# One product per tile of 32 keys: the operands of a level stage laid together in one tile

## The chip, the cores and the metric

The kernel runs on one core of a Trainium2 chip. The metric is the device time of one launch in microseconds (us), the median of several runs. Five engines work at once, each through its own queue in order: PE multiplies matrices (its weight loads are listed apart, as PEld), DVE, ACT and POOL do elementwise work, SP starts transfers (DMA).

## The reference, cut to what matters

The model has one layer: RMSNorm, a combined input projection, a causal pooling branch and a gated linear recurrence, a gated merge, an output projection, then a gated feed-forward part. The change lies in the recurrence alone, which is computed for 4 heads of 128 channels over 2048 positions:

```
q = silu(zq);  f = lb + (1 - lb) * sigmoid(zf);  k = 1 - f;  v = zi
S_t = diag(f_t) S_{t-1} + k_t v_t^T
o_t = S_t^T q_t
```

Written over a chunk of positions this is `attn[t, s] = sum_c q[t, c] * k[s, c] * prod(f[s+1..t, c])` for s <= t, then `o = attn v` plus a term from the state at the chunk's start.

## The kernel before, in words

All large products are done in float32 that is split in a high and a low part (three products for one), and in two-level form with seven partial products P1 to P7 instead of eight. The sequence is worked in two rounds (`b` = 0 and 2) of 1024 positions, as two halves of `TB` = 512. A round is a mixer (projections, recurrence, pooling, merge) and a feed-forward part (up projection, convolution, down projection). The weights come through a stream of raw tiles that SP loads; ACT casts the high part and DVE subtracts the low part. In round 0 the kernel also makes the sums of weights that the seven-product form needs, in DRAM, by large accumulating transfers (class `Sums`).

The recurrence of one head and one half is `hgrn_task`, a Python generator. It is stepped by `tick`, once for every 6 large products that the kernel emits, so its instructions stand between those of the projections; `yield AHEAD` puts 3 ticks between making the operands and using them. The two halves of a head run as a pair and share every place: a **group** below means the products of both halves at one place. There are 4 heads in each of 2 rounds, so 8 pairs. A scheduler sets the final order on every engine; `in_turn` pins a group to its place in PE's stream.

A half has `NT` = 4 chunks of 128 positions. Instead of dividing by decays, `hgrn_task` builds the 128x128 matrix of a chunk in four **level stages** (`hh` = 1, 2, 8, 32). At each, queries are multiplied by the decay up to a block's border (`d`, `f` in the profile) and keys by the decay behind it; `q`, `k` and `d` are updated in place for the next stage. Stages 1, 2 and 8 fill the diagonal tiles of 32 keys (`GK` = 32, `NG` = 4 tiles per chunk); stage 32 fills the blocks between the tiles.

For each stage `operands` gives two tiles: `qn` with the near queries in two parts of 64 columns a chunk, and `qf` with one further part. `products` multiplies, for each chunk, each part (`s`) and each key tile `g`, 32 columns of keys (the weights) with 32 columns of `qn`, or with 16 of `qf`. The four key tiles write four different quarters of the PSUM partitions, `ps[g * GK : g * GK + GK]`. After that `put` copies the wanted elements under a mask into `at` (DVE), and stage 32 copies blocks with ACT. Products of this part are plain float32; the profile lists two matmuls and two weight loads for each.

All these tiles, like nearly everything else in SBUF, come from one pool `slots` of 77 buffers of 512 (528) columns. A buffer is given out again when its last reader is done, which can be a transfer that stores it.

Of the kernel before, what the change touches and what calls it, by code (L numbers as in the profile page):

```python
# [11 lines left out]
F32 = mybir.dt.float32  # L12
# [3 lines left out]
ALU = mybir.AluOpType  # L16
AX = mybir.AxisListType

P = 128
# [38 lines left out]

M_ORDER = (0, 4, 1, 5, 2, 6, 3, 7)

N_SLOTS = 77
N_RUN = 3
N_HEADS = 2
GO_AT = 3
# [21 lines left out]
def tile_trunk(  # L86
# [20 lines left out]
    rawp = ctx.enter_context(tc.tile_pool(name="rawp", bufs=N_RAW))  # L107
    opsp = ctx.enter_context(tc.tile_pool(name="opsp", bufs=N_OPS))
    slots = ctx.enter_context(tc.tile_pool(name="slots", bufs=N_SLOTS))
    dram = ctx.enter_context(tc.tile_pool(name="dram", bufs=1, space=bass.MemoryType.DRAM))  # L110
    banks = ctx.enter_context(tc.tile_pool(name="banks", bufs=8, space=bass.MemoryType.PSUM))

    def slot(name, cols=TB, dt=F32):
        return slots.tile([P, cols], dt, tag="s", name=name, padded_shape=[P, 528])
# [513 lines left out]
    def setup_task():  # L628
        scratch = [hist.rearrange("p a b -> p (a b)")[:, :64], uhist.rearrange("p a b -> p (a b)")]

        def mask_of():
            scratch.reverse()
            return scratch[0]

        keys = [(h, h, 0, h) for h in (1, 2, 8)]
        keys += [(8 * h + t, 2 * h, t * h, h) for h in (2, 8) for t in range(2)]
        for key, x, off, w in keys:
            nb = 64 // x
            mf = mask_of()
# [20 lines left out]
        masks[0] = m8.unsqueeze(2)  # L660
# [339 lines left out]
    def hgrn_task(b, h, d, q, vd, zd, od):  # L1000
# [20 lines left out]
        def products(hh, near, far):  # L1021
            x = GK // 2
            pa_ = bank(f"pl{b}_{h}_{hh}", NT * 3 * x)
            ps = pa_.rearrange("p (c x) -> p c x", c=NT)
            for c in range(NT):
                for s in range(2):
                    for g in range(NG):
                        o = ps[g * GK : g * GK + GK, c]
                        ins = pe.matmul(
                            o[:, 2 * x :] if s else o[:, : 2 * x],  # L1030
                            ks[:, c * P + g * GK : c * P + g * GK + GK],
                            far[:, c, g * x : g * x + x] if s else near(c, g),
                            start=True, stop=True)
                        if not (c or g or s):
                            in_turn(ins)
# [12 lines left out]
        qn, qf = operands(1)  # L1048
        act.copy(qn.rearrange("p c s x -> p (c s x)"), q)
        dve.tensor_tensor(qf, qo, do, ALU.mult)  # L1050
        dve.tensor_tensor(qe, qe, de, ALU.mult)
        dve.tensor_tensor(qo, qf, de, ALU.mult)
        yield AHEAD
        flat = qn.rearrange("p c s x -> p c (s x)")
        ps = products(1, lambda c, g: flat[:, c, g * GK : g * GK + GK], qf)
        yield 2
        dve.copy_predicated(ac, masks[0].rearrange("p x o -> p o x").to_broadcast([P, NT, GK]),
                            ps[:, :, :GK])
# [5 lines left out]
        for hh in (2, 8, 32):  # L1064
# [4 lines left out]
            qn, qf = operands(hh)  # L1069
            half = qn[:, :, 1].rearrange("p c (b t h) -> p c b t h", t=2, h=hh)  # L1070
            act.copy(qn[:, :, 0].rearrange("p c (b h) -> p c b h", h=hh),
                     qv.rearrange("p c (b t h) -> p c b t h", t=2, h=hh)[:, :, :, 1, :])
            act.copy(half[:, :, :, 0, :], q5[:, :, :, 2, :])
# [3 lines left out]
            f4 = qf.rearrange("p c (b h) -> p c b h", h=2 * hh)  # L1077
            dve.tensor_tensor(f4, qn[:, :, 1].rearrange("p c (b h) -> p c b h", h=2 * hh),
                              d5[:, :, :, 1, 0:1].to_broadcast(full), ALU.mult)
            dve.tensor_tensor(q2, f4, d5[:, :, :, 0, 0:1].to_broadcast(full), ALU.mult)  # L1080
            yield AHEAD
            if hh < GK:
                x = GK // 2
                ps = products(hh, lambda c, g: qn[:, c, :, g * x : g * x + x], qf)
                yield 1
                put(halves(hh), hh, ps[:, :, :x], hh)
                for t in range(2):
                    put(halves(2 * hh), 8 * hh + 1 - t, ps[:, :, (1 + t) * x : (2 + t) * x], 2 * hh)
            else:
                for g in range(NG - 1):  # L1090
                    r = slice(g * GK, g * GK + GK)
                    act.copy(av[r, :, r], ac[r])
                pa_ = bank(f"pl{b}_{h}_{hh}", NT * 96)
                ps = pa_.rearrange("p (c x) -> p c x", c=NT)
                for c in range(NT):
                    for g, to, w in ((0, slice(0, 32), qn[:, c, 0, :32]), (1, slice(0, 64), qn[:, c, 1]),
                                     (2, slice(0, 32), qn[:, c, 0, 32:]), (0, slice(32, 96), qf[:, c])):
                        ins = pe.matmul(ps[g * GK : g * GK + GK, c, to],
                                        ks[:, c * P + g * GK : c * P + g * GK + GK], w,
                                        start=True, stop=True)  # L1100
                        if not c and not g and not to.start:
# [897 lines left out]
```

## Time and profile before

| what | value |
|---|---|
| time, median of 3 runs (range) | 2491.97 us (2491.5 to 2494.51) |
| time of the profiled execution | 2491.93 us |
| span of that execution | 2490.1 us, granted PE clock 0.997 |
| busy: PE, PEld, DVE, ACT, POOL | 2464.5, 2004.7, 1924.1, 1233.2, 780.5 us |
| matmuls on line 1029 (stages 1, 2, 8) | 1536 of 32 columns, 1536 of 16 columns |
| matmuls on line 1098 (stage 32) | 384 from qn, 128 from qf |

The time around the span is 1.8 us. In rows of the profile, `L1029` is a line of the kernel, `pl<-qn,k` means that the instruction writes `pl` and reads `qn` and `k` (numbers of buffers left out), and `128x32` is partitions by elements of the moving operand. A row of a timeline has the start, the time from the first start to the last end, and how many instructions were merged; in square brackets stands the time that the engine was idle before it, and what ended that.

### The profile page before, as it was taken

The page shows a single profiled execution, that of the slowest core. Times are in us where ns is not written, and L with a number is a line of the kernel's source. Part 1 is how long each engine was busy: PE and PEld are TensorE (multiplying, and loading weights), DVE is VectorE, ACT ScalarE, POOL GpSimd, SP SyncE. Part 2 cuts the span into 40 slices and gives each one's busy share as a digit, 9 for nine tenths or more (in the row PEclk, how much of TensorE's full clock was granted, in tenths as well). Part 3 has the DMA queues.
Part 4 walks back from the last instruction along what each step waited for, and adds up shares of the span by engine and source line. Part 5 has one row for each costly group of instructions (what it writes and reads, how often), then busy time and mean ns, then how long its engine had stood idle before and what let it go on. Part 6 is the DMA issues. An engine that isn't in the chain of part 4 may idle for free.

```text
span 2490.1 us, 41224 instructions
## 1 busy us (share of the span) xinstructions
PE 2464.5 (99%) x14372; PEld 2004.7 (81%) x14372; DVE 1924.1 (77%) x3318; ACT 1233.2 (50%) x2344; POOL 780.5 (31%) x1090
## 2 busy tenths in 40 slices
PE   9999999999999999999999999999999999999998
PEld 7877787887888888888888888887888888888887
DVE  7767666988899777885596766769979887778755
ACT  6535444434545545554464455453365554445534
POOL 5343352502354334461240101213033433335410
PEclk9999999999999999999999999999999999999999
DMA  8878778687898879997444343457443444447852
GB/s 274 273 198 268 213 219 249 205 251 250 200 260 232 232 222 245 262 364 249 131 157 154 114 145 120 141 161 245 147 138 123 157 145 143 148 136 248 319 165 100
DMA packets 257711, 498.03 MB, mean 200 GB/s; under 512 B 26912, under 2 KB 47520, under 8 KB 257184
## 3 DMA queue, kind: packets, MB, share of 16 engines
q1 hardware_dynamic: 189872, 317.53, 38.9%
q0 software_dynamic: 42656, 112.74, 17.7%
q10 hardware_dynamic: 24976, 65.13, 7.5%
q8 instruction: 113, 1.85, 0.3%
q14 instruction: 94, 0.77, 0.1%
HBM read 383.63 MB, written 189.27 MB: 230 GB/s over the span
## 4 chain that ended last, share of the span: by engine, by line
PE 80%; DVE 3%; DMA 2%; issue 1%; ACT 0%; POOL 0%; SPq 0%; ACTq 0%; DVEq 0%; POOLq 0%
PE dn_P L152 17%; PE up_Z L152 15%; PE up_V L152 10%; PE up_X L152 10%; PE wo_P L152 5%; PE pb L152 3%; PE gr_X L152 2%; PE gr_V L152 2%; PE io_Z L152 1%; PE gr_Z L152 1%; PE gr_Y L152 1%; PE gr_W L152 1%; PE io_V L152 1%; PE fr_X L152 1%; PE fr_V L152 1%; DVE ops L249 1%
## 5 line engine op out<-in xcount | busy, mean ns | idle before, releaser
L248 ACT CAST ops<-raw 128x512 fp32r<-128x512 f32 x792 | 487.5, 620 | 798.6 <-PE dn_P L152 180.2
L249 DVE TENSOR_TENSOR ops<-raw,ops 128x512 fp32r<-128x512 f32 x792 | 590.4, 749 | 239.3 <-ACT ops L248 229.9
L1733 DVE SCALAR_TENSOR_TENSOR e<-h,cols,e 128x512 f32<-128x512 f32 x176 | 143.1, 818 | 30.5 <-ACT e L1731 25.9
L1731 ACT ACTIVATE e<-h,cols 128x512 f32<-128x512 f32 x176 | 142.2, 814 | 25.5 <-DVE h L1181 18.8
L1736 DVE SCALAR_TENSOR_TENSOR e<-h,cols,e 128x512 f32<-128x512 f32 x176 | 133.7, 769 | 2.5
L996 POOL DMA_DIRECT2D g_P<-dg_P x154 | 84.5, 550 | 159.8 <-PE dn_P L152 113.5
L1302 POOL TENSOR_TENSOR gf_P<-e,e 128x512 f32<-128x512 f32 x44 | 61.5, 1400 | 150.4 <-DVE e L1742 96.2
L470 POOL TENSOR_TENSOR raw<-raw,raw 128x512 f32<-128x512 f32 x36 | 49.9, 1386 | 110.2 <-DVE ops L249 95.6
L1302 POOL TENSOR_TENSOR gf_P<-gf_P,e 128x512 f32<-128x512 f32 x44 | 59.1, 1343 | 72.1 <-DVE e L1742 71.6
L1726 POOL COPY h<-h 128x2 f32<-128x2 f32 x88 | 40.3, 470 | 117.0 <-DVE h L1180 107.4
L1740 ACT ACTIVATE e<-e 128x512 f32<-128x512 f32 x88 | 55.6, 632 | 38.0 <-DVE e L1736 37.8
L1728 POOL COPY hist<-h 128x2 f32<-128x2 f32 x88 | 35.9, 408 | 117.6 <-DVE h L1181 115.8
L1181 DVE TENSOR_TENSOR h<-up_u,up_V 128x512 f32<-128x512 f32 x88 | 60.0, 682 | 10.2 <-PE up_V L152 9.7
L1442 POOL TENSOR_TENSOR q<-q,qs 128x512 f32<-128x512 f32 x16 | 22.4, 1401 | 125.0 <-ACT qs L1441 125.0
L1277 DVE TENSOR_TENSOR x<-x,wo_P 128x512 f32<-128x512 f32 x88 | 55.9, 680 | 5.9 <-PE wo_P L152 5.6
L1277 DVE TENSOR_TENSOR ac<-ac,dn_P 128x512 f32<-128x512 f32 x72 | 47.1, 681 | 16.3 <-PE dn_P L152 16.1
L1475 ACT ACTIVATE gt<-gt,cols 128x512 f32<-128x512 f32 x48 | 34.8, 725 | 42.8 <-DVE gt L1181 41.5
L1221 ACT COPY up_e<-up_X 128x512 f32<-128x512 f32 x44 | 25.9, 588 | 59.3 <-PE up_X L152 56.4
L718 POOL TENSOR_SCALAR ro<-so 128x4 f32<-128x4 f32 x16 | 5.0, 311 | 156.3 <-ACT sq L1154 156.1
L1726 POOL COPY h<-hist 128x2 f32<-128x2 f32 x88 | 44.5, 513 | 28.5 <-DVE m_T42l L685 28.5
L1756 POOL DMA_DIRECT2D dg_P<-gf_P x88 | 50.7, 576 | 8.1 <-POOL gf_P L1302 7.4
L1616 POOL TENSOR_TENSOR ya<-ya,gl 128x512 f32<-128x512 f32 x24 | 36.7, 1552 | 26.2 <-DVE ya L1613 14.8
(1328 smaller groups left out, 8021.4 us busy)
## 6 DMA issues: line engine op xcount, KB each, us to landing
g_P<-dg_P POOLq DMA_DIRECT2D x154, 256.0 KB, 5.9
raw<-in_w_up_t SPq DMA_DIRECT2D x132, 256.0 KB, 3.0
raw<-in_w_in_t SPq DMA_DIRECT2D x98, 256.0 KB, 3.5
dg_P<-gf_P POOLq DMA_DIRECT2D x88, 256.0 KB, 3.9
dg_P<-e SPq DMA_DIRECT2D x66, 256.0 KB, 3.4
raw<-in_w_dn SPq DMA_DIRECT2D x66, 256.0 KB, 3.9
x<-in_x SPq DMA_DIRECT2D x64, 256.0 KB, 4.6
gd<-gt ACTq DMA_DIRECT2D x64, 256.0 KB, 3.4
```

Source lines behind the costliest of these rows:

```text
L152: count[1] = pe.matmul(*args, **kw)
L248: self.mark = act.copy(hi, v)
L249: low = self.low = dve.tensor_tensor(lo, v, f32(hi), ALU.subtract)
L996: eng.dma_start(t, d)
L1181: return dve.tensor_tensor(dst, t, ps, ALU.add if how == "add" else ALU.subtract)
L1277: dve.tensor_tensor(t, t, ps[j], ALU.add if sg > 0 else ALU.subtract)
L1302: pin(eng.tensor_tensor(t, x0, x1, op))
L1726: pool.tensor_copy(h[:, 0:2], hist[:, mt] if hf == 0 else hs[s, 0][:, TB : TB + 2])
L1731: in_turn(act.activation(t, h[:, 2:], AF.Identity, bias=col(o_cb + mt), scale=col(o_cw + 4 * MF + mt)))
L1733: in_turn(second(dve.scalar_tensor_tensor(t, h[:, 1 : 1 + TB], col(o_cw + 2 * MF + mt), t, ALU.mult, ALU.add)))
L1736: dve.scalar_tensor_tensor(t, h[:, 0:TB], col(o_cw + mt), t, ALU.mult, ALU.add)
L1740: in_turn(act.activation(g, g, AF.Silu))
```

## The change

`operands` now gives one tile `qm` with three parts of 64 columns per chunk, from a pool of its own with 3 buffers of 768 columns; `slots` goes from 77 buffers to 73. The parts are in such an order that the columns for key tile `g` are 16 of each part. `products` issues one matmul of 48 columns per chunk and key tile, where there were two of 32 and 16. In stage 32 the far part lies behind the first two, so key tile 0 takes 96 neighbouring columns in one product: three products per chunk where there were four.

With the layout some elementwise work changes shape. In stage 1 even and odd queries go to different parts, so ACT's one copy of 512 columns becomes two strided copies of 256, and the masked copy reads the product in another order. In stage 32 one ACT copy of 256 columns becomes two of 128. The other copies and multiplications write other places with the same sizes.

```diff
-N_SLOTS = 77
+N_SLOTS = 73
+N_QM = 3
...
+    qmp = ctx.enter_context(tc.tile_pool(name="qmp", bufs=N_QM))
...
         def operands(hh):
-            near = slot(f"qn{b}_{h}_{hh}").rearrange("p (c s x) -> p c s x", c=NT, s=2)
-            far = slot(f"qf{b}_{h}_{hh}")[:, : NT * 64].rearrange("p (c x) -> p c x", c=NT)
-            return near, far
+            t = qmp.tile([P, NT * 192], F32, tag="qm", name=f"qm{b}_{h}_{hh}")
+            return t.rearrange("p (c s x) -> p c s x", c=NT, s=3)
...
-                for s in range(2):
-                    for g in range(NG):
-                        o = ps[g * GK : g * GK + GK, c]
-                        ins = pe.matmul(
-                            o[:, 2 * x :] if s else o[:, : 2 * x],
-                            ks[:, c * P + g * GK : c * P + g * GK + GK],
-                            far[:, c, g * x : g * x + x] if s else near(c, g),
-                            start=True, stop=True)
+                for g in range(NG):
+                    ins = pe.matmul(ps[g * GK : g * GK + GK, c],
+                                    ks[:, c * P + g * GK : c * P + g * GK + GK],
+                                    qm[:, c, :, g * x : g * x + x], start=True, stop=True)
...
-        act.copy(qn.rearrange("p c s x -> p (c s x)"), q)
-        dve.tensor_tensor(qf, qo, do, ALU.mult)
+        qm = operands(1)
+        act.copy(qm[:, :, 0], qe)
+        act.copy(qm[:, :, 1], qo)
+        dve.tensor_tensor(qm[:, :, 2], qo, do, ALU.mult)
...
+            if hh < GK:
+                act.copy(near, qh)
+            else:
+                for i in range(2):
+                    act.copy(near[:, :, 1 - i], qh[:, :, i])
...
-                    for g, to, w in ((0, slice(0, 32), qn[:, c, 0, :32]), (1, slice(0, 64), qn[:, c, 1]),
-                                     (2, slice(0, 32), qn[:, c, 0, 32:]), (0, slice(32, 96), qf[:, c])):
+                    flat = qm[:, c].rearrange("p s x -> p (s x)")
+                    for g, (at, w) in enumerate(((96, 96), (0, 64), (64, 32))):
```

Two places show how it stands in the queues. The first is PE's queue at stage 2 of head 0 in round 0. `gr_0_X<-x_f5h` and its like are large products of the projection; `pl_0_2` is the PSUM bank of this stage, once for each half; `x4` counts neighbouring rows alike. Before (each pair of rows of one half stands four times):

```order
L152 MATMUL gr_0_X<-x_f5l,ops_1445 128x512
L152 MATMUL gr_0_X<-x_f5h,ops_1445 128x512
L1029 MATMUL pl_0_2_1649<-qn_0_2_1593,k_0_1451 32x32 x4
L1029 MATMUL pl_0_2_1649<-qf_0_2_1594,k_0_1451 32x16 x4
...
L1029 MATMUL pl_0_2_1682<-qn_0_2_1604,k_0_1464 32x32 x4
L1029 MATMUL pl_0_2_1682<-qf_0_2_1605,k_0_1464 32x16 x4
...
L152 MATMUL gr_0_X<-x_f6h,ops_1445 128x512
```

In the changed kernel the same place of PE's queue reads:

```order
L154 MATMUL gr_0_X<-x_f5l,ops_1448 128x512
L154 MATMUL gr_0_X<-x_f5h,ops_1448 128x512
L1028 MATMUL pl_0_2_1618<-qm_0_2_1564,k_0_1454 32x48 x16
L1028 MATMUL pl_0_2_1635<-qm_0_2_1574,k_0_1467 32x48 x16
L154 MATMUL gr_0_X<-x_f6h,ops_1448 128x512
```

The group stands between the same two large products; its 64 products of two sizes are now 32 of one. Over the whole program all other PE instructions keep their order, and two of the 32 groups stand one product later.

The second place is ACT's queue where the operands of stage 1 of head 0 are made, for both halves. `CAST ops` is the high part of a weight tile, `f`, `k` and `qs` belong to the recurrence, the `DMA` rows start transfers for the sums of weights. Before:

```order
L248 CAST ops_1490<-raw_1103 128x512
L1009 ACTIVATE k_0_1451<-f_0_1388 128x512
L1437 ACTIVATE f_0_1434<-f_0_1434 128x512
L1049 COPY qn_0_1_1456<-q_0_1408 128x512
L1008 ACTIVATE f_0_1434<-f_0_1434,lbt 128x512
L248 CAST ops_1578<-raw_1120 128x512
L325 DMA su0s_1358<-in_w_up_t 512x1x512
L1009 ACTIVATE k_0_1464<-f_0_1434 128x512
L1049 COPY qn_0_1_1469<-q_0_1363 128x512
L1221 COPY gr_0_e_1481<-gr_0_X 128x512
```

In the changed kernel ACT's queue at that place reads:

```order
L250 CAST ops_1493<-raw_1106 128x512
L1011 ACTIVATE k_0_1454<-f_0_1391 128x512
L1439 ACTIVATE f_0_1437<-f_0_1437 128x512
L1046 COPY qm_0_1_1459<-q_0_1411 128x4x64
L1047 COPY qm_0_1_1459<-q_0_1411 128x4x64
L1010 ACTIVATE f_0_1437<-f_0_1437,lbt 128x512
L1046 COPY qm_0_1_1472<-q_0_1366 128x4x64
L1047 COPY qm_0_1_1472<-q_0_1366 128x4x64
L250 CAST ops_1549<-raw_1123 128x512
L327 DMA su0s_1361<-in_w_up_t 512x1x512
L1011 ACTIVATE k_0_1467<-f_0_1437 128x512
L1223 COPY gr_0_e_1484<-gr_0_X 128x512
```

Two copies stand where one stood, and the second half's copies have moved ahead of a weight cast and of `k`.

More of the change, by code (lines that the diff above doesn't have):

```diff
@@ L1016, in operands, with products @@
         def operands(hh):
[L1017 to L1021 removed]
+            t = qmp.tile([P, NT * 192], F32, tag="qm", name=f"qm{b}_{h}_{hh}")
+            return t.rearrange("p (c s x) -> p c s x", c=NT, s=3)
+        def products(hh, qm):
             x = GK // 2
@@ L1047, in hgrn_task @@
         de, do = (dv.rearrange("p c (b t) -> p c b t", t=2)[:, :, :, t] for t in range(2))
-        qn, qf = operands(1)
-        act.copy(qn.rearrange("p c s x -> p (c s x)"), q)
-        dve.tensor_tensor(qf, qo, do, ALU.mult)
+        qm = operands(1)
+        act.copy(qm[:, :, 0], qe)
+        act.copy(qm[:, :, 1], qo)
+        dve.tensor_tensor(qm[:, :, 2], qo, do, ALU.mult)
         dve.tensor_tensor(qe, qe, de, ALU.mult)
-        dve.tensor_tensor(qo, qf, de, ALU.mult)
+        dve.tensor_tensor(qo, qm[:, :, 2], de, ALU.mult)
         yield AHEAD
-        flat = qn.rearrange("p c s x -> p c (s x)")
-        ps = products(1, lambda c, g: flat[:, c, g * GK : g * GK + GK], qf)
+        ps = products(1, qm)
         yield 2
-        dve.copy_predicated(ac, masks[0].rearrange("p x o -> p o x").to_broadcast([P, NT, GK]),
-                            ps[:, :, :GK])
+        dve.copy_predicated(ac.rearrange("p c (b t) -> p c b t", t=2),
+                            masks[0].to_broadcast([P, NT, GK // 2, 2]),
+                            ps[:, :, :GK].rearrange("p c (t b) -> p c b t", t=2))
         put(halves(1), 1, ps[:, :, GK:], 1)
@@ L1068, in hgrn_task @@
             q2 = qv.rearrange("p c (b t h) -> p c b t h", t=2, h=2 * hh)[:, :, :, 1, :]
[L1069 to L1072, printed above, removed]
+            qm = operands(hh)
+            qh = qv.rearrange("p c (b t h) -> p c b t h", t=2, h=hh)[:, :, :, 1, :]
+            near = qm[:, :, 1].rearrange("p c (b h) -> p c b h", h=hh)
+            half = qm[:, :, 0].rearrange("p c (b t h) -> p c b t h", t=2, h=hh)
+            if hh < GK:
[3 more added lines that the diff above has]
+                    act.copy(near[:, :, 1 - i], qh[:, :, i])
             act.copy(half[:, :, :, 0, :], q5[:, :, :, 2, :])
@@ L1076, in hgrn_task @@
             full = [P, NT, nb, 2 * hh]
[L1077 to L1080, printed above, removed]
+            f0, f1 = (qm[:, :, s].rearrange("p c (b h) -> p c b h", h=2 * hh) for s in (0, 2))
+            dve.tensor_tensor(f1, f0, d5[:, :, :, 1, 0:1].to_broadcast(full), ALU.mult)
+            dve.tensor_tensor(q2, f1, d5[:, :, :, 0, 0:1].to_broadcast(full), ALU.mult)
             yield AHEAD
@@ L1083, in hgrn_task @@
                 x = GK // 2
-                ps = products(hh, lambda c, g: qn[:, c, :, g * x : g * x + x], qf)
+                ps = products(hh, qm)
                 yield 1
-                put(halves(hh), hh, ps[:, :, :x], hh)
+                put(halves(hh), hh, ps[:, :, x : 2 * x], hh)
                 for t in range(2):
-                    put(halves(2 * hh), 8 * hh + 1 - t, ps[:, :, (1 + t) * x : (2 + t) * x], 2 * hh)
+                    put(halves(2 * hh), 8 * hh + 1 - t, ps[:, :, 2 * t * x : (2 * t + 1) * x], 2 * hh)
             else:
@@ L1095, in hgrn_task @@
                 for c in range(NT):
-                    for g, to, w in ((0, slice(0, 32), qn[:, c, 0, :32]), (1, slice(0, 64), qn[:, c, 1]),
-                                     (2, slice(0, 32), qn[:, c, 0, 32:]), (0, slice(32, 96), qf[:, c])):
[L1098 to L1101, printed above, removed]
+                    flat = qm[:, c].rearrange("p s x -> p (s x)")
+                    for g, (at, w) in enumerate(((96, 96), (0, 64), (64, 32))):
+                        ins = pe.matmul(ps[g * GK : g * GK + GK, c, :w],
+                                        ks[:, c * P + g * GK : c * P + g * GK + GK],
+                                        flat[:, at : at + w], start=True, stop=True)
+                        if not (c or g):
                             in_turn(ins)
```

6 lines of the change are left out of this document (3 added, 3 removed).

## The prediction

> **What bounds the kernel now.** I read the page's busy times and chain first, then the waits of PE, then the two mixers beside each other, then single groups. The page, parts 1, 3 and 4:
>
> ```profile
> PE 2464.5 (99%) x14372; PEld 2004.7 (81%) x14372; DVE 1924.1 (77%) x3318; ACT 1233.2 (50%) x2344; POOL 780.5 (31%) x1090
> q8 instruction: 113, 1.85, 0.3%
> PE 80%; DVE 3%; DMA 2%; issue 1%; ACT 0%; POOL 0%; SPq 0%; ACTq 0%; DVEq 0%; POOLq 0%
> ```
>
> PE sets the end: what is taken off its stream comes off the time, as long as others keep up. Its longest waits (total, times, longest), and the two mixers as stretches (length, then busy time and count for PE, PEld, DVE, ACT and POOL, granted clock, DMA share, GB/s):
>
> ```profile
> PE pl L1029 <- issue: 4.7, 3, 2.9
> PE gr_X L152 <- issue: 3.1, 1, 3.1
> PEld pl L1029 <- ACT qn L1049: 1.5, 2, 0.9
> ```
>
> ```profile
> 100.00:420.00 320.00, 308.75 (x3079) 249.92 (x3078) 219.52 (x525) 151.45 (x341) 121.86 (x117) 0.98 0.82 234
> 1350.00:1640.00 290.00, 290.00 (x3045) 238.63 (x3045) 198.46 (x515) 145.05 (x327) 36.71 (x52) 1.00 0.41 129
> ```
>
> Nearly the same PE work, and the groups among it, runs without a gap in the second mixer; in the first, where the DMA engines are busy twice as much, PE idles 11 us and its clock is below full. So there are two things to price: the groups themselves, in both mixers, and the stops around them, in the first.
>
> **The groups.** The start of one group (24 of these, 256 matmul and load records each):
>
> ```profile
> 122.02 0.40 PE L152 MATMUL gr_Z<-x_T23h,ops 128*128 128x512 f32 x1
> 122.49 0.40 PE L152 MATMUL gr_Z<-x_T23h,ops 128*128 128x512 f32 x1
> 122.82 0.27 PE L1029 MATMUL pl<-qn,k 128*32 128x32 f32 x8
> 122.90 0.23 PE L1029 MATMUL pl<-qf,k 128*32 128x16 f32 x8
> 122.97 0.25 PE L1029 MATMUL pl<-qn,k 128*32 128x32 f32 x8
> 123.03 0.23 PE L1029 MATMUL pl<-qf,k 128*32 128x16 f32 x8
> 123.09 0.22 PE L1029 MATMUL pl<-qn,k 128*32 128x32 f32 x2
> ```
>
> Two large products take 0.47 us, so 0.235 us is the price of one. In the group eight matmuls of 16 columns take as long as eight of 32: 0.19 us for three eights from 122.90 to 123.09, 63 ns for one, 32 ns for a set of four, one per key tile. The width does not pace these matmuls; something fixed per matmul does. Stage 32 shows what width costs once it does pace. Key tile 0 takes two matmuls of 32 and two of 64 per chunk there; the rows of `qf` are its wide ones:
>
> ```profile
> 1393.75 0.22 PE L1098 MATMUL pl<-qf,k 128*32 128x64 f32 x1
> ...
> 1393.81 0.22 PE L1098 MATMUL pl<-qf,k 128*32 128x64 f32 x1
> ...
> 1394.10 0.22 PE L1098 MATMUL pl<-qf,k 128*32 128x64 f32 x1
> ```
>
> A 64-column matmul holds its tile for 60 ns, and two chunks take 0.35 us, 175 ns each, which leaves (175 - 120) / 2 = 28 ns for one of 32. Between 28 and 60 the new one of 48 columns lies at 44 ns. A group had 8 chunks x 4 matmuls per key tile x 32 ns = 1.02 us; now 8 x 2 x 44 = 0.70 us. That saves 0.32 us. The whole group is longer than this pace; two clean groups of the second mixer, busy time of line 1029 alone:
>
> ```profile
> 1370.80:1373.80 3.00, 1.31 (x128) 1.21 (x128) 1.00 0.28 93
> 1378.80:1381.80 3.00, 1.35 (x128) 1.25 (x128) 1.00 0.52 148
> ```
>
> Less 0.2 us for the last matmul (the 0.22 in the rows), 1.13 us over 32 sets is 35 ns, and then 1.13 - 0.70 = 0.43 us is saved. I take 0.36, nearer the pace that the rows show directly: 24 x 0.36 = **8.6 us**, with ends 24 x 0.32 = 7.7 and 24 x 0.43 = 10.3. The unknown is whether four key tiles of 48 columns stream side by side as freely. The 32-column sets ran 128 columns in 32 ns, 4 per ns; the new ones need 192 in 44, 4.4 per ns. If 4 were the limit a set takes 48 ns and the saving falls by 16 x 4 ns = 0.06 a group to 7.2 us, my lower end.
>
> [...]
>
> Stage 32: key tile 0 goes from 2 x 28 + 2 x 60 to two matmuls of 96 columns, at 1 ns per column from 60 up 92 ns each: 184 against 175 ns a chunk. Eight groups of 8 chunks: +0.6 us at worst; if a wider matmul only adds its 0.83 ns per column (28 ns for 32 less a fixed 1.5), -0.4. I take 0.
>
> **The stops.** The two longest that nothing in the profile releases ("issue"), with what follows:
>
> ```profile
> 139.38 0.18 PE L1029 MATMUL pl<-qf,k 128*32 128x16 f32 x1
> 142.44 0.30 PE L1029 MATMUL pl<-qf,k 128*32 128x16 f32 x6 [2.87 <-issue]
> 142.67 0.80 PE L152 MATMUL gr_V<-x_B222h,ops 128*128 128x512 f32 x1
> 145.79 0.40 PE L152 MATMUL ur_X<-x_f0l,ops 128*128 128x512 f32 x1
> 395.46 0.39 PE L152 MATMUL gr_X<-x_f1h,ops 128*128 128x512 f32 x1
> 398.96 0.80 PE L152 MATMUL gr_X<-x_f1l,ops 128*128 128x512 f32 x1 [3.11 <-issue]
> 403.82 0.63 PE L152 MATMUL gr_Z<-x_T21h,ops 128*128 128x512 f32 x1
> ```
>
> I read these as PE waiting for its own instructions. Queue q8 brings 1.85 MB in 113 packets, 16 KB each; 2 x 14372 records over 113 is 254, so a packet is 256 instructions of 64 bytes with the waits among them. Counts of PE's records at the four issue stops:
>
> ```profile
> 0.00:139.40 139.40, 134.59 (x984) 110.41 (x985) 109.43 (x206) 79.73 (x158) 58.29 (x112) 1.00 0.84 267
> 0.00:216.80 216.80, 209.12 (x1744) 171.08 (x1745) 164.46 (x342) 116.04 (x243) 91.92 (x146) 0.99 0.84 252
> 0.00:294.55 294.55, 284.57 (x2504) 232.19 (x2504) 211.94 (x463) 154.84 (x332) 117.06 (x169) 0.99 0.83 246
> 0.00:395.48 395.48, 382.53 (x3392) 311.57 (x3392) 288.21 (x628) 199.51 (x433) 159.59 (x211) 0.99 0.83 242
> ```
>
> That is 1969, 3489, 5008 and 6784 records, 177, 161, 144 and 128 past a whole packet, with separate wait instructions still to add. Adding those four counts' waits (15, 31, 48, 64 in the trace) puts all four at the same place of a packet, three quarters. Large products use a packet in 128 x 0.235 = 30 us; a group uses one in 1.2 us, and in the first mixer the next comes late. After the change a group uses half a packet. Halving the groups' records in the trace, the shortest time from asking to needing grows from 7 to about 10 us, most to 14: only the latest packet here (12 us) could still stop PE, if it fell there.
>
> So these go: 4.7 + 3.1 = 7.8 us of waiting. After the two long ones large products run at half pace: 7 in 3.12 us (142.67 to 145.79) instead of 1.64, and 11 in 4.86 (398.96 to 403.82) instead of 2.58: 1.5 + 2.3 = 3.8 us. Together **11.6 us**, from 0 (see the rivals) to this.
>
> [...]
>
> One more stop is for data:
>
> ```profile
> 283.50 0.27 PE L1029 MATMUL pl<-qn,k 128*32 128x32 f32 x8
> 285.59 0.28 PE L1029 MATMUL pl<-qf,k 128*32 128x16 f32 x8 [1.82 <-DVE qf L1078]
> 286.44 0.80 PE L152 MATMUL gr_X<-x_f4l,ops 128*128 128x512 f32 x1
> 289.14 0.40 PE L152 MATMUL gr_X<-x_f6l,ops 128*128 128x512 f32 x1
> 285.11 0.42 DVE L1078 TENSOR_TENSOR qf<-qn,f 128x256 f32<-128x256 f32 x1 [4.40 <-DMA wb<-cw]
> ```
>
> DVE waited 4.4 us to write `qf`, because its buffer still held a `cw` tile on its way to DRAM. `qm` has buffers of its own, used by nothing that is stored, and three suffice for two halves: the oldest is read out a stage earlier. Gone: 1.8 + (2.70 - 6 x 0.235) = **3.1 us**.
>
> **What it adds.** ACT's copies, all medians from one view of each line:
>
> ```profile
> L1049 ACT COPY qn<-q x16: 600/605/622, 118.9 to 1604.3; 128x512 f32<-128x512 f32 x16
> L1071 ACT COPY qn<-q x48: 388/402/444, 123.2 to 1621.5; 128x256 f32<-128x256 f32 x48
> L1073 ACT COPY qn<-q x48: 292/295/336, 123.6 to 1621.8; 128x128 f32<-128x128 f32 x48
> ```
>
> Stage 1: 2 x 402 - 605 = 0.2 us more per half; stage 32: 2 x 295 - 402 = 0.19. ACT is half idle, and three ticks (18 x 0.235 = 4.2 us) lie between operands and group. Without that cover they cost up to 16 x 0.39 = 6.2 us; PE waited for these copies 1.5 us in one group (row above), so I take **+0.5**. ACT queues the second half's `k`, PE's weights, behind them: in the same 0.5. DVE keeps its count and sizes: 0 behind its 23% idle time; the masked copy reads PSUM in another order, at worst +50% of 0.3 us on 16, also hidden.
>
> `slots` loses four buffers, while the stages no longer take up to four of it (two halves with two tiles each). Other tiles now inherit the buffers that are being stored, gates above all, and DVE or ACT may wait as for `qf`. Between 0 and what went, 3.1: I take **+1.5**.
>
> Sum against the profiled execution, 2491.93 (0.04 from the median): -8.6 - 11.6 - 3.1 + 0.5 + 1.5 = -21.3, **2470.6 us**.
>
> **The rivals.** (1) The stops move: DVE, ACT and the loads catch up during them, and without them PE waits for these instead. For it, DVE waited too while PE stood at 285; against it, DVE is only 69% busy in the first mixer. Left is the groups' gain: 2491.9 - 8.6 + 0.5 = 2483.8. (2) Forty-eight columns in three pieces stream no faster than two matmuls did: against it the 60 ns of the 64-column ones. Stops gone alone: 2491.9 - 11.6 - 3.1 + 2.0 = 2479.2. (3) Nothing comes through, within 0.2% (5 us, about what can be told from no change). (4) Slower, through 73 buffers in the down projection, whose loads already wait for a buffer:
>
> ```profile
> POOL g_P L996 <- PE dn_P L152: 113.5, 38, 18.8
> ```
>
> If each of these 38 waits comes one step of 12 products later (12 x 0.235 = 2.8 us) and PE has no lead, 107 us are lost; it decides from 26 / 38 = 0.7 us each, and at 1 us the time is 2491.9 - 21 + 38 = 2508.5. Against it, PE waits nowhere in that stage now, and the order there is unchanged.
>
> **How the numbers follow.** Main case 0.67 (own range 2462 to 2478: groups 7.2 to 10.3, new waits 0 to 6, and the 2 us of other data waits that may go as well), rival 1 0.13, rival 2 0.10, rival 3 0.05, rival 4 0.05. The range 2460 to 2484 holds the main case and most of 1 and 2. Faster 0.90, same 0.05, slower 0.05.
>
> **What would show it.** A clean group of 64 matmuls busy about 0.95 us instead of 1.33; no "issue" wait before `pl` or `gr_X`; the clock at 1.00 in 100 to 420; 100 instruction packets on q8 instead of 113. I am wrong if the groups still take 1.2 us, or if PE's waits turn up under ACT or DVE.

## The result and the profile after

Before 2492.57 us (median of 4, 2491.5 to 2494.51), after **2472.14 us** (median of 4, 2470.74 to 2472.64): a ratio of 0.9921 with a 95% interval from 0.9909 to 0.9934, 20 us saved. The profiled execution took 2470.74 us, 21.2 less than the one before. The forecast was 2470.6.

The page after, parts 1, 3 and 4 (busy time, instruction queue, chain):

```profile
PE 2448.3 (99%) x12708; PEld 1986.6 (80%) x12708; DVE 1921.2 (78%) x3318; ACT 1237.0 (50%) x2376; POOL 783.6 (32%) x1090
q8 instruction: 100, 1.64, 0.3%
PE 91%; DVE 4%; DMA 1%; issue 1%; ACT 1%; POOL 0%; SPq 0%; ACTq 0%; DVEq 0%; POOLq 0%
```

PE still sets the end, with 1664 records of matmuls fewer and 13 packets of instructions fewer. The two mixers as stretches, the columns as before:

```profile
100.00:420.00 320.00, 316.57 (x2359) 256.20 (x2358) 228.96 (x543) 159.61 (x379) 129.57 (x122) 1.00 0.87 249
1350.00:1640.00 290.00, 290.00 (x2263) 237.76 (x2262) 200.30 (x527) 147.97 (x356) 38.38 (x54) 1.00 0.43 138
```

In the first mixer PE idles 3.4 us instead of 11.3, at full clock (1.00 granted, 0.98 before), though DMA is busier than before (0.87 against 0.82). What PE waits for now, from its list of waits over the whole run (`x_t` and the first constants are waits of the first 15 us):

```profile
PE x_t L750 <- DVE x_xs L744: 3.1, 4, 1.1
PE pl L1028 <- ACT k L1011: 1.8, 2, 1.0
...
PE gr_V L154 <- DVE gt L1183: 1.3, 1, 1.3
PE pl L1028 <- DVE qm L1081: 1.0, 1, 1.0
PE pa_V L154 <- DVE ya L1615: 0.9, 3, 0.5
PE pl L1100 <- DVE qm L1081: 0.7, 1, 0.7
...
PE pa_Y L154 <- DVE mf2T41l L687: 0.2, 1, 0.2
```

No row ends in "issue". All are waits for data, none over 1.3 us but that for the first constants (1.7, as before). The rows of the kernel before that answer to these, without the stops shown ahead:

```profile
PE pl L1029 <- DVE qf L1078: 2.4, 2, 1.8
PE x_t L748 <- DVE x_xs L742: 2.2, 4, 0.9
...
PE pl L1029 <- ACT qn L1049: 0.8, 1, 0.8
...
PE pa_V L152 <- DVE ya L1613: 0.5, 2, 0.4
```

A clean group, then one of stage 32, with the large products at their sides:

```profile
1353.55 0.40 PE L154 MATMUL gr_Z<-x_T23h,ops 128*128 128x512 f32 x1
1353.88 0.89 PE L1028 MATMUL pl<-qm,k 128*32 128x48 f32 x64
1354.70 0.51 PE L154 MATMUL gr_V<-x_T10h,ops 128*128 128x512 f32 x1
...
1374.18 0.39 PE L154 MATMUL ur_Z<-x_T21h,ops 128*128 128x512 f32 x1
1374.49 1.51 PE L1100 MATMUL pl<-qm,k 128*32 128x96 f32 x48
1375.93 0.50 PE L154 MATMUL ur_Z<-x_T21l,ops 128*128 128x512 f32 x1
```

The group is busy 0.89 us, where before it was 1.31 to 1.35. From its first start to its last it takes 682 ns (1168 before, medians over all 24). The records of one key tile start 42.5 ns apart; before they started 32 to 34 ns apart, with a step of 42 to 53 several times a group, 36 in the mean.

### The profile page after: what moved, and what is told of

Its sections match the earlier page's. It is cut to its first block, busy times and chain, and to the rows that moved or that the text cites. A ratio compares the mean times of both kernels' runs of the same rounds, so it can differ in the third digit from the quotient of the medians.

```text
span 2468.7 us, 37997 instructions
## 1 busy us (share of the span) xinstructions
PE 2448.3 (99%) x12708; PEld 1986.6 (80%) x12708; DVE 1921.2 (78%) x3318; ACT 1237.0 (50%) x2376; POOL 783.6 (32%) x1090
## 3 DMA queue, kind: packets, MB, share of 16 engines
q8 instruction: 100, 1.64, 0.3%
## 4 chain that ended last, share of the span: by engine, by line
PE 91%; DVE 4%; DMA 1%; issue 1%; ACT 1%; POOL 0%; SPq 0%; ACTq 0%; DVEq 0%; POOLq 0%
PE dn_P L154 17%; PE up_Z L154 15%; PE up_V L154 10%; PE up_X L154 10%; PE wo_P L154 6%; PE gr_V L154 3%; PE gr_X L154 3%; PE pb L154 3%; PE io_Z L154 3%; PE io_V L154 2%; PE gr_Z L154 2%; PE fr_V L154 1%; PE gr_W L154 1%; PE fr_X L154 1%; PE gr_Y L154 1%
## 5 line engine op out<-in xcount | busy, mean ns | idle before, releaser
L998 POOL DMA_DIRECT2D g_P<-dg_P x154 | 83.7, 545 | 173.7 <-PE dn_P L154 125.5
L1183 DVE TENSOR_TENSOR h<-up_u,up_V 128x512 f32<-128x512 f32 x88 | 60.1, 683 | 10.4 <-PE up_V L154 9.9
```

Of the source, the lines that this page charges most:

```text
L998: eng.dma_start(t, d)
L1183: return dve.tensor_tensor(dst, t, ps, ALU.add if how == "add" else ALU.subtract)
```

## The experiments

Two explanations of the stops stood against each other. **A**: PE stops because a group uses up a packet of 256 instructions in about a microsecond and the next one comes late. **B**: the stops come from the operand tiles in the shared pool, so from buffers and transfers. A third question was what PE still waits for after the change. Ratios are to the kernel before, run on the same chip, with 95% intervals.

**1. Products split again, on the new tile.** Each key tile is multiplied twice, as before, but the layout, the pool and the elementwise work are those of the changed kernel.

```diff
-                for g in range(NG):
-                    ins = pe.matmul(ps[g * GK : g * GK + GK, c],
-                                    ks[:, c * P + g * GK : c * P + g * GK + GK],
-                                    qm[:, c, :, g * x : g * x + x], start=True, stop=True)
+                for s in range(2):
+                    for g in range(NG):
+                        o, r = ps[g * GK : g * GK + GK, c], qm[:, c, :, g * x : g * x + x]
+                        ins = pe.matmul(o[:, 2 * x :] if s else o[:, : 2 * x],
+                                        ks[:, c * P + g * GK : c * P + g * GK + GK],
+                                        r[:, 2] if s else r[:, :2], start=True, stop=True)
...
```

> The changed kernel with its operand tile, but each tile of 32 keys again multiplied twice per chunk (32 and 16 columns) in stages 1 to 8, and four products per chunk in the last stage. Theory A (the stops of PE for its own instructions come from groups that use up a packet of 256 instructions in about 1.1 us): the products cost 24 x 0.455 + 8 x 0.07 = 11.5 us more, and the four stops with their half pace come back at 3/4 of a packet, 7 to 12 us: 2491 to 2496 us. Theory B (the stops came from the operand buffers in the shared pool of slots, which this kernel no longer uses for them): only the 11.5 us come back and PE waits nowhere for its instructions: 2483.6 us, 2481 to 2485.

Measured 2482.0 us (5 runs, 2479.67 to 2484.46), 0.9962 of before (0.995 to 0.9974). The time is in B's range, but the trace has A's stops. PE's waits, and the longest place:

```profile
PE gr_X L154 <- issue: 3.2, 2, 2.4
...
PE pl L1030 <- issue: 0.7, 1, 0.7
```

```profile
390.18 0.40 PE L154 MATMUL gr_X<-x_f1h,ops 128*128 128x512 f32 x1
393.01 0.50 PE L154 MATMUL gr_X<-x_f2h,ops 128*128 128x512 f32 x1 [2.43 <-issue]
```

There are 3.9 us of stops, half of before. This execution (2484.46) is 13.7 us longer than the profiled one of the changed kernel. Without their waits the groups make 11.5 of that (24 x 0.455 and 8 x 0.07), the stops 3.9, and one stretch at half pace about 1.7, from 371 to 374 us, behind a wait of 0.97 us for `k`; the waits for data are 2.8 us shorter. That adds up to 14.3, so 0.6 is not accounted for. By the medians, halving the products on the new tile is worth 9.9 us, about half of the change's 20, and the tile with its pool the other half; neither theory had that. Halving the products in the shared pool was not run.

**2. Own pools, everything else as before.** The two kinds of operand tile get three buffers each; `slots` has 73.

```diff
-            near = slot(f"qn{b}_{h}_{hh}").rearrange("p (c s x) -> p c s x", c=NT, s=2)
-            far = slot(f"qf{b}_{h}_{hh}")[:, : NT * 64].rearrange("p (c x) -> p c x", c=NT)
+            near = qnp.tile([P, NT * 128], F32, tag="qn", name=f"qn{b}_{h}_{hh}")
+            far = qfp.tile([P, NT * 64], F32, tag="qf", name=f"qf{b}_{h}_{hh}")
...
```

> The kernel before, with its two products per tile, but the operand tiles of 128 and of 64 columns per chunk come from two pools of their own (three buffers each) and the shared pool has 73. Theory A: the stops for instructions stay as they are (four in the first mixer, about 8 us, and the half pace behind them), only the stop at 283.5 us for a buffer still being stored goes: 2489.5 us, 2486.5 to 2493. Theory B: with the buffers apart the stops go as well, 3.1 + 11.6 us: 2478 us, 2475 to 2481.

Measured 2484.21 us (11 runs, 2481.4 to 2490.34), 0.9978 (0.9969 to 0.9987), that is 3 to 8 us less. PE's waits:

```profile
PE pl L1034 <- issue: 3.7, 2, 2.8
...
PE gr_X L156 <- issue: 1.5, 1, 1.5
```

The wait for `qf` at 283.5 us is gone, as both theories had it. The stops are there, 5.2 us in place of 7.8, one of them at another group. B falls: without a shared buffer in the operands PE still waits for instructions. But the pool counts for more than A's 3.1 us: when buffers and transfers move, the stops get longer or shorter. The eleven runs are not alike (seven took 2481.4 to 2485.0 us, four 2488.7 to 2490.3), the profile is of one of the seven, and what divides them is open.

**3 and 4. A shift by part of a packet.** Sixteen small matmuls behind the first warm-up products, in the kernel before and in the changed one; the order of all else on the engines stays.

```diff
             warm(WARM[0])
+            tiny = bank("tiny", P)
+            for _ in range(16):
+                pe.matmul(tiny[:GK, :16], ident[:, :GK], ident[:, :16], start=True, stop=True)
```

> The kernel before with 16 tiny matmuls (32 x 16, 128 matmul and load records) behind the first warm-up products, so that every later instruction of PE stands half a packet further on; the order on the engines is otherwise the same. Theory A: stops for instructions stay at 3/4 of a packet, so each comes 128 records earlier in the program (in the other half of its group or in the group ahead), and near 139, 216, 294 and 392 us there are still some; total of the stops 4 to 14 us, time 2492.6 -4 / +6. Theory B: the stops stay at the same products as before, whatever their place in a packet; time 2492 to 2495.

They are two records of a matmul and two of a load each, so 64 records and a quarter of a packet, not the 128 that I had written. Measured on the kernel before: 2489.76 us (12 runs, 2482.41 to 2493.63), 0.9987 (0.9978 to 0.9995). Records of PE up to the last stop, in the stretch from the start, and the stop:

```profile
0.00:386.21 386.21, 378.38 (x3392) 308.42 (x3392) 284.90 (x619) 198.09 (x431) 157.89 (x211) 1.00 0.84 247
```

```profile
388.69 0.21 PE L1032 MATMUL pl<-qf,k 128*32 128x16 f32 x2 [2.30 <-issue]
```

Before the shift the stop at 395 us came after 3392 matmuls and 3392 loads, behind the group, in the products of `gr_X`. Now it comes after 3392 and 3392 again, but 64 records earlier in the program, inside the group. It stays at the place in the packet and not at the product: that is what A says, and theory B had it the other way. The profiled execution (2483.95) is one of the three short ones, nine of the twelve took 2488.7 to 2493.6 us; its list has only this stop and one of 0.3 us.

> The changed kernel with 16 tiny matmuls more at the start (64 records: a quarter of a packet, as the run of the same shift on the kernel before showed). If the changed kernel has no stops because its groups leave enough time in every packet: none here either, 2471 to 2475 us. If it was only lucky in where its packets end: stops of 3 to 10 us come back, 2475 to 2483 us.

Measured on the changed kernel: 2471.54 us (4 runs, 2470.09 to 2472.59), 0.9917 (0.9902 to 0.9932), no stop. So the changed kernel has none at a second place of its packets' ends either; other places were not run.

**5. Less traffic in the first mixer.** The kernel before without the 40 accumulating transfers of the weight sums on POOL's queue; it leaves them out, so its output differs.

```diff
                 if add:
-                    in_turn(pool.dma_start(self.t[g, dst], x, accum_op=ALU.add))
+                    yield SUM_LAG
+                    continue
```

> The kernel before without the additions of the weight sums (40 accumulating transfers of 1 MB on POOL's queue, 25 % of the DMA engines' time in the first mixer); the sums, and what is made with them later, have other values. Theory A: with DMA at about 0.6 in the first mixer the packets come in time, so the four stops and the half pace behind them go: 2480 us, 2477 to 2485. Theory B: the stops stay, 2490 to 2494 us.

Measured 2478.56 us (4 runs, 2476.11 to 2479.85), 0.9944 (0.9929 to 0.9959). The first mixer, and PE's waits:

```profile
100.00:420.00 320.00, 316.29 (x3149) 257.28 (x3148) 221.51 (x539) 156.38 (x355) 110.18 (x107) 0.99 0.60 202
```

```profile
PE pl L1031 <- issue: 2.2, 2, 1.7
...
PE gr_X L152 <- issue: 0.2, 1, 0.2
```

The stops fall from 7.8 to 2.4 us, the time by 14 us (10 to 18). As A has it in the time; the stops are shorter, not gone.

**6 to 9. More traffic, in the second mixer.** There a packet is used up as fast (PE runs 320 instructions in 7.1 us at the shortest, in both mixers of the kernel before), and no stop was seen. A first pair of runs added 150 copies of 256 KB from DRAM to DRAM, but nothing held them back, and ACT sent them out at the start, where PE waited for its weights (`io_V` for ACT's `ops`: 37.9 us in the kernel before, 36.9 in the changed one; no such row stands in their lists without the copies).

```diff
+    def extra():
+        for i in range(150):
+            e = dram.tile([P, 512], F32, tag=f"ex{i}", name=f"ex{i}")
+            act.dma_start(e, x[(i % 16) * P : (i % 16) * P + P, 0:512])
+            yield 1 + i % 2
...
```

> The kernel before with 150 more copies of 256 KB from DRAM to DRAM, issued by ACT all through the second mixer (about 1370 to 1660 us), where DMA was 0.41 busy and no stop for instructions was seen although the groups use up packets as fast as in the first mixer. Theory A (a packet is used up faster than a new one comes when DMA is busy): stops for instructions turn up in the second mixer, at 3/4 of a packet, 3 to 12 us of them with the half pace: 2495 to 2506 us. Theory B (they come from the operand buffers in the shared pool, or a busy DMA alone does not make them): none there; 2490 to 2496 us.

> The changed kernel with the same 150 copies in its second mixer. Theory A: no packet is used up there in under 9.4 us, against 7.1 us in the kernel before, so there are no stops for instructions or one short one: 2471 to 2476 us. Rival: under a load like this packets come late for the changed kernel too: stops of 3 to 12 us there, 2476 to 2485 us.

Measured 2596.25 us on the kernel before and 2578.46 on the changed one; both far off for that reason, and no test of the second mixer. In the first, the kernel before had three stops (5.4 us), at 1969, 3489 and 5008 records as in the first profile; the changed one had none. Then with each copy held behind ACT's work of the moment (`with tc.issue_after(stream.mark.ins)`):

> The kernel before with 150 copies of 256 KB from DRAM to DRAM, now each held behind ACT's work of the moment, so that they lie in the second mixer (in the run before they went out at the start). DMA there should go from 0.41 busy to 0.7 or more. Theory A: stops for instructions turn up there, near 1380 to 1395 and 1452 to 1466 us, where a packet was used up in 7.1 to 8.0 us without a stop in the kernel before: 2 to 10 us of them. Theory B: none there. The time itself also holds what the copies cost other transfers, so the trace decides: stops without any semaphore, at one place of a packet.

> The changed kernel with the same copies in its second mixer. Theory A: the tightest packet there takes 9.4 us, so no stop for instructions, or one under 1 us. Rival: stops as in the kernel before under this load, 2 to 10 us.

Measured 2500.95 us (4 runs; 1.0039, 1.0025 to 1.0053) and 2480.97 us (4 runs; 0.9959, 0.9944 to 0.9975). The second mixer of the kernel before, and PE's waits over the whole of it:

```profile
1350.00:1640.00 290.00, 290.00 (x3037) 238.67 (x3036) 196.36 (x514) 144.04 (x324) 36.29 (x52) 1.00 0.74 229
```

```profile
PE gr_X L152 <- issue: 4.9, 1, 4.9
PE pb L152 <- DVE pa_u L1238: 4.4, 1, 4.4
PE pl L1039 <- issue: 4.2, 3, 2.4
```

All four stops lie in the first mixer, at the four known places; the changed kernel has none under this load. In the second, at 0.74 and nearly the first's bandwidth (229 GB/s against 234), there is none: that a busy DMA and a fast group are enough, as A was written down, is wrong. The copies cost time at `pb`, where PE waits for DVE's `pa_u` (4.4 us, and 5.9 in the changed kernel; without the copies there is no such wait). I read this as the data for `pb` standing behind the copies; the lists show the wait alone.

**10. The long transfers.** Twelve times a copy of 1 MB and two accumulating transfers of 1 MB on POOL's queue, in the second mixer of the kernel before.

```diff
...
+                s = v[:, (i + n) % 8 * 2048 : (i + n) % 8 * 2048 + 2048]
+                if n:
+                    in_turn(pool.dma_start(e, s, accum_op=ALU.add))
+                else:
+                    with tc.issue_after(stream.mark.ins):
+                        act.dma_start(e, s)
...
```

> The kernel before with transfers of 1 MB like those of the weight sums in its second mixer: twelve times a copy from DRAM to DRAM and two accumulating transfers on POOL's queue. The copies of 256 KB brought DMA to 0.74 busy there and made no stop; the packets started 2.9 us (median) after they were due, against 4.2 us in the first mixer. Theory A1 (it is the long transfers of the sums, the accumulating ones above all, behind which a packet waits): the packets start 3.5 to 5 us after they are due, and stops come at the tight packets (7.1 to 8.0 us, near 1380 to 1395, 1452 to 1466 and 1530 us), 2 to 10 us: 2493 to 2506 us. Theory A2 (long transfers do no more than short ones; something else in the first mixer makes the packets late): none, 2489 to 2495 us.

Measured 2499.64 us (7 runs, 2494.12 to 2503.99), 1.0039 (1.0028 to 1.0051).

```profile
1350.00:1640.00 290.00, 289.04 (x3035) 237.71 (x3034) 196.44 (x513) 143.46 (x324) 55.22 (x74) 1.00 0.89 245
```

```profile
PE pl L1045 <- issue: 4.4, 3, 2.6
...
PE gr_X L152 <- issue: 3.1, 1, 3.1
```

The list again has only the four stops of the first mixer; the time went into waits for data (17.8 us in the list, against 10.4 in that of the kernel before). But the packets did come later. In the traces a packet starts on q8 at the earliest 1.1 us after PE has begun the 128th instruction of a packet (its wait instructions counted), and where PE had to stop it goes on past the 192nd of the next one 2.2 to 2.6 us after that start, 2.3 in most cases. I call the first span the delay, and the time in which PE runs those 320 instructions the window; a stop comes where delay + 2.3 us is more than the window (without the stop itself).

| kernel, stretch | delay, median (longest) | shortest window | stops |
|---|---|---|---|
| before, first mixer | 4.3 (9.7) us | 7.1 us | 7.8 us |
| before without the accumulating transfers, first | 3.2 (6.9) | 7.1 | 2.4 |
| before, second mixer | 2.3 (4.5) | 7.1 | 0 |
| with copies of 256 KB, second | 2.9 (5.7) | 7.2 | 0 |
| with transfers of 1 MB, second | 4.0 (7.0) | 7.1 | 0.3 (see below) |
| after, first mixer | 4.2 (8.8) | 9.2 | 0 |

The rule was read off these traces, but it holds through all of them. In the eight profiles with two products per tile it asks for 29 stops, of 0.1 to 5.3 us, and right behind that 192nd instruction PE's starts stand still at each of the 29, by a length that differs from the rule's by 0.3 us at most. In the first profile it asks for 3.0, 0.7, 1.5 and 3.3 us; 3.1, 0.7, 1.6 and 3.5 pass from one start to the next. In the six profiles with one product it asks for none. (The lists of waits have 26 of the 29; the others are too short for them, as the products before them are still running.)

A1 is right on the delay (4.0, expected 3.5 to 5) and wrong on the stops, but for one. At 1461 us a delay of 5.1 us met a window of 7.1; by the rule that is a stop of 0.3 us, and the weight loads stand still there for a moment:

```profile
1461.05 0.14 PEld L1045 LDWEIGHTS pl<-qf,k 128*32 128x32 f32 x4
1461.38 0.11 PEld L1045 LDWEIGHTS pl<-qf,k 128*32 128x32 f32 x2 [0.19 <-issue]
```

At the other tight packets the delays were 1.4 to 4.5 us; the longer ones met wide windows. In the first mixer the same tight packets are hit in nearly every run: those asked for near 132 and 387 us started 7.8 and 9.7 us later in the first profile, 7.6 and 9.8 in this one. Why these two stays open. By the same rule the changed kernel could still stop, if its longest delay (8.8 + 2.3 = 11.1 us) fell on its shortest window (9.2); in none of the six profiles with one product did it.

**11. Keys ahead of the copies; 12. and the products later.**

```diff
-        act.activation(ks, d, AF.Identity, bias=1.0, scale=-1.0)
+        kdone = act.activation(ks, d, AF.Identity, bias=1.0, scale=-1.0)
...
-        act.copy(qm[:, :, 0], qe)
-        act.copy(qm[:, :, 1], qo)
+        behind(act.copy(qm[:, :, 0], qe), kdone)
+        behind(act.copy(qm[:, :, 1], qo), kdone)
...
-            yield AHEAD
+            yield AHEAD + (hh < GK)
```

> The changed kernel, but ACT may not run the two operand copies of stage 1 before the activation that makes the keys of the same half. If PE's new waits under that activation (1.8 us at L1028, 3.5 us counting weight loads) come from the copies standing ahead of it, they go: 2470 us, 2468 to 2471. If the activation is late for another reason, or another wait takes their place: 2472, 2471 to 2474.

The first part alone: 2470.78 us (5 runs, 2469.03 to 2472.86), 0.9917 (0.9904 to 0.993), not to be told from the changed kernel. The waits under `k` are gone, and others stand in their place:

```profile
PE pl L1028 <- ACT qm L1047: 1.2, 2, 1.0
PE pl L1028 <- DVE qm L1081: 1.0, 1, 1.0
PE pl L1100 <- DVE qm L1081: 1.0, 1, 1.0
...
PE pl L1028 <- DVE f L1116: 0.8, 2, 0.6
```

I read this as ACT and DVE being late with their work as a whole, and the order as deciding only which instruction came last; no run shows that by itself. With the products of stages 2 and 8 one tick (six large products) later as well:

> The changed kernel with the keys of a half made ahead of its operand copies, and the products of stages 2 and 8 six matmuls (1.4 us) later behind their operands. If PE's remaining waits in the first mixer (five of 0.8 to 1.4 us under DVE's multiplication for the operands) come from products that stand too near behind it, three or four go: 2467 us, 2465 to 2470. If DVE has too much to do there, the waits move along: 2470.8, 2469 to 2473.

Measured **2464.39 us** (4 runs, 2463.75 to 2467.46), 0.9894 (0.9879 to 0.9908): the fastest of all, 7.7 us below the changed kernel (whose interval begins at 0.9909). PE's waits, without those of the start:

```profile
PE pl L1028 <- ACT qm L1047: 2.0, 2, 1.2
...
PE po L1151 <- DVE ss L1141: 1.3, 1, 1.3
PE pl L1100 <- DVE qm L1081: 0.6, 1, 0.6
...
PE pb L154 <- DVE oTs_1l L687: 0.2, 1, 0.2
```

The waits under DVE's `qm` in stages 2 and 8, under `gt` and in the pooling part are gone. More went than the three or four waits that I had counted on. The two lists differ by 4.0 us and the profiled executions by 6.7, so the rest is open; the later products alone were not run, so the shares of the two edits are open too.

## Why the prediction was right

Step by step, against the profiled executions:

- **The groups, -8.6 (7.2 to 10.3): measured -10.9.** A clean group costs PE's stream 1.474 us before and 1.020 after, 24 x 0.455. This term was too small, and beyond its own end. I had the new pace nearly right (44 ns; 42.5 measured), but the old one too low: 32 ns is the step between two sets in a row, and the group holds several steps of 42 to 53, so 36 in the mean. The estimate from the whole group (0.43 us) was the better one, and I had passed it over. The doubt on 4 columns per ns was unfounded: 192 columns in 42.5 ns are 4.5.
- **Stage 32, 0 (-0.4 to +0.6): -0.57**, 8 x 0.07 (1.702 to 1.631 us a group), a little beyond its lower end. The -0.4 doesn't follow from its own figures: 96 columns at 0.83 ns and 1.5 are 81 ns, two of them 162 against 175 a chunk, which is -0.8 over 64 chunks. In the changed kernel's trace the records of 96 columns start 82.5 ns apart (165 for two in a row) and those of 48 columns 42.5, so 0.83 ns for each further column; the 1.5 was an estimate, and these two steps leave 2.5.
- **The stops, -7.8, and the half pace behind them, -3.8: gone, all of it.** The cause held in its main part: the place in the packet (run 4 above all), and no stop in any of the six profiles with one product per key tile, two of them under added load, against 2 to 4 stops in the list of each of the eight with two, and the rule of delay and window, which gives their lengths. What failed is "in the first mixer the next comes late" because DMA is busy: with 0.74 and 0.89 in the second mixer none came but one of 0.3 us. In these traces a stop needs a long delay at a short window (delay + 2.3 us above it). The change works on the window, not on the delay, which was 4.3 us before and is 4.2 after.
- **The stop at 283.5 us, -3.1: gone.** Run 2 showed that pools of their own are enough for that; in its one profile the stops are shorter as well.
- **ACT's copies and new waits, +0.5 and +1.5: measured +4.0.** By the two lists, waits for data in the mixers were 0.6 + 0.8 + 0.5 = 1.9 us before, without the 1.8 at 283.5, and are 5.9 after: `k` 1.8, `qm` 1.7, `gt` 1.3, the pooling part 1.1. Of ACT I had put `k` "in the same 0.5"; its two waits alone are 1.8. DVE's masked copy of stage 1, for which I had put +50% at worst with no run behind it, took 296 ns in the median against 294 before. DVE's own lateness I put at 0, behind its idle time (69% busy in the first mixer). I read it as rival 1 in small: the stops had been the time in which DVE caught up; no run shows that by itself. By the prediction's own sign ("if PE's waits turn up under ACT or DVE") this term was wrong.
- At the start and the end of the stages PE waits 0.6 us more (`x_t` 3.1 against 2.2, less `io_Z`).

The sum: -10.9 - 0.6 - 11.6 - 3.1 + 4.0 + 0.6 = -21.6, against -21.2 measured. Predicted -21.3: the groups came out 2.9 us better with stage 32, the new waits 2.6 worse, so the total was nearer than its parts. That it came within 0.2 us is luck.

The rivals. Stops that only move (1) would have left 2484: 4.6 of the 14.7 us came back. Forty-eight columns at 60 ns (2): 42.5. Nothing (3): no. The down projection with 73 buffers (4): POOL's loads of `g_P` wait 125.5 us for PE in place of 113.5, and PE waits nowhere there. (Its 2508.5 should be 2508.9 by the figures beside it; nothing rests on that.) Where the 20 us come from is told by runs 1 and 2 differently than by my sum. Both keep two products per tile and have operand pools of their own, and 3.9 and 5.2 us of the stops are left, against 7.8; so the pool, too, seems to take part of them away, and what halving the products in the shared pool would leave is open.

In the eight profiles with two products per tile PE stood at 3 to 5 of the 113 packets of a profile, each time 320 instructions behind the 128th of a packet, and for up to 9.1 us in all; at the others there was no stop for instructions.

## What to carry to other kernels

Count instructions per microsecond, not only their time: a burst of 256 short records can cost several microseconds more than it lasts (up to 4.9 us here), and halving the records removed that where the work stayed the same. What to compare, by the traces of these runs, is the time in which PE runs 320 instructions (here from 7.1 us) with the delay of a packet (up to 9.8) and 2.3 us. Where such stops go, the engines behind them may lose the time in which they caught up (my reading of the 4.0 us of new waits), so price the next waits (here DVE and ACT) at more than zero; with the keys made first, six large products more between operands and products then gave another 0.3%.

## What the runs showed of the hardware

Four column tiles of 32 keys side by side take 16 and 32 moving columns at one pace, 32 to 34 ns a record in the kernel before, and 48 at 42.5 ns in the changed one.

Runs of the kernel before reached from 2487.67 to 2495.61 us (23 runs, on the chip of runs 1 to 3). So the stops of one profile are one draw: sums of stops in single profiles, as in runs 1, 2 and 5, may differ by some us without a cause in the kernel. Whether the changed kernel spreads less can't be told: its four runs spread by 1.9 us, the first four of the kernel before by 3.0.

Half pace behind a stop doesn't go by its length alone. After 2.77 us in the kernel with its own pools the large products ran on at 0.23 us each:

```profile
216.87 0.22 PE L1034 MATMUL pl<-qn,k 128*32 128x32 f32 x1 [2.77 <-issue]
...
217.43 0.39 PE L156 MATMUL gr_V<-x_B221h,ops 128*128 128x512 f32 x1
217.66 0.39 PE L156 MATMUL gr_V<-x_B222h,ops 128*128 128x512 f32 x1
```

After 2.30 us in the shifted kernel they ran at 0.41 us each:

```profile
389.79 0.61 PE L152 MATMUL gr_V<-x_B222l,ops 128*128 128x512 f32 x1
390.20 0.63 PE L152 MATMUL gr_V<-x_B222h,ops 128*128 128x512 f32 x1
```

In the kernel before the stretches at half clock (0.50 granted) last 3.4 us or 6.8 and start at 142.3, 285.7 and 398.3 us, multiples of 3.41 us apart. Cut at that step (its place is taken from each trace's record of the clock), the stop in the kernel with its own pools is divided over two stretches, with PE busy 1.75 and 2.30 of 3.41 us, and that in the shifted kernel lies in one, with 1.11 (the second number is PE's busy time, the third from the end the granted clock):

```profile
212.35:215.76 3.41, 1.75 (x121) 1.27 (x119) 3.41 (x14) 0.60 (x2) 0.00 (x0) 1.00 0.94 163
215.76:219.17 3.41, 2.30 (x19) 1.92 (x20) 3.41 (x15) 2.11 (x6) 0.00 (x0) 1.00 1.13 224
```

```profile
386.38:389.79 3.41, 1.11 (x24) 0.94 (x24) 3.41 (x15) 1.22 (x3) 0.74 (x1) 1.00 0.50 164
389.80:393.21 3.41, 3.41 (x10) 2.63 (x9) 3.41 (x12) 0.62 (x1) 1.06 (x1) 0.50 0.69 254
```

So where a stop falls seems to count, but the busy share of a stretch doesn't settle it either: behind 1.91 us busy in run 1 the clock was half (at 371 us), behind 1.64 in the shifted kernel (277.2 to 280.6) it was full.
